# Transposes grouped, two jobs moved to ScalarE, warm matmuls among the first four: a hybrid decoder block in float32

## The chip, the core and the metric

The kernel runs on one core of a Trainium2 chip. The metric is the device time of one execution in microseconds (us). Before the change three runs gave 397.14, 397.4 and 397.8, with a median of 397.4. Below, PE is TensorE, DVE is VectorE, ACT is ScalarE, POOL is GpSimd and SP is SyncE, which issues most transfers.

## What is computed

One decoder layer on 256 tokens of width 1024, in float32. A norm feeds five projections: q, k, v (8 heads of 128), u (512 wide, the input of a state space model) and two gates. Attention is causal within one block of 256. The state space model is a complex diagonal scan with 64 states in each of 32 groups, followed by a gated linear unit (glu). Both branches are gated, summed and projected (wo), and a squared-ReLU MLP (up, down) follows.

```
h = rms_norm(x, norm_mix_g);  q, k, v, u, g = split(h @ w_in)
q, k = rotary(q), rotary(k)
o_a = softmax(mask(q k^T * 128**-0.5)) v
y   = gelu(scan(lambda, B u) C + d_skip * u);  val, gt = split(y @ w_glu);  o_b = val * sigmoid(gt)
x = x + (sigmoid(g_a) * o_a + sigmoid(g_b) * o_b) @ w_out
h = rms_norm(x, norm_mlp_g);  x = x + relu(h @ w_up)**2 @ w_down
return rms_norm(x, norm_final_g)
```

## The kernel before, in words

Every product with a weight is done as three matmuls in the 32-bit replicated format: a weight block `raw` arrives by a transfer on SP's queue, ACT casts it to `hi` (line 83), DVE subtracts to get `lo` (line 84), and PE multiplies hi by the high part of the activations, hi by their low part and lo by their high part (`mm3`, `tok_mm`). There are five raw, four hi and four lo buffers. So each stage is a pipeline SP, ACT, DVE, PE. The stages follow each other: warm matmuls on zeros (`hot`, line 151), the projection u in eight steps k (lines 161 to 183), v, then q, k and the gate for four pairs of heads with attention and the state space model between them (the string `ORDER`), glu, wo, up, down, and the final norm.

Nothing in the source fixes the order of instructions across these parts. A scheduler with a simulated timeline sorts each engine's instructions, with priorities (`tc.high_priority`), and the engines then run their lists strictly in that order. An instruction that waits holds up everything behind it in its engine's list. So an edit in one place can reorder the lists elsewhere.

Names that the later text uses. In the u stage, `xgh` (ACT) and `xgl` (DVE) are the high and low part of the scaled input of a step k, and `hi_u`, `lo_u` the parts of its weights. `par` is a small transfer (128 rows of 60 numbers) with parameters of the state space model; the chain of 128x16 operations that starts on it (`s`, in `prepare`) runs on DVE. `sq` are the squares for the first norm, summed on DVE and then over partitions by the `ms` matmuls; `rs_half` waits for the inverse root that POOL computes. `tables(m)` makes the cosine and sine tables of the scan from a high and a low part of the phase; the low part is added by line 520. `place` (line 455) copies the 16-wide blocks `ab` into the wide matrix `Bs`, whose transposes are `bt`. `s` on PE is the scores' tile (line 307), `pr` the probabilities and `pt` their transposes. `mt` are the transposes of a glu group.

At the end of wo, `x2t` is the residual stream (line 690). For its two column halves c it is transposed (`xt`, line 692, 8 transposes for each half), then ACT writes the scaled high part `x2h` (line 696) and DVE the low part `x2l` (line 697) of each block m, which the matmuls of up read. ACT also sums the squares of x2t (line 700, twice). The two banks of `xt` are used by c=0 and then by c=1, so the second set of transposes waits until x2h and x2l of the first are made.

Of the kernel before, what the change touches and what calls it, by code (L numbers as in the profile page):

```python
# [34 lines left out]

RAW, HI, LO = 5, 4, 4
SPLIT_PRIO = 800
HEAT = 7
RSP = 600
ATT_PRIO = 300  # L40
LAST = 4
# [7 lines left out]
def build(ctx, tc, dr, out):  # L49
# [45 lines left out]
    def behind(ins, others, reason="table set"):  # L95
        for o in others:
            tc.add_manual_dep(ins, o.name, mybir.DependencyInfo(
                mybir.DependencyClass.NoSync, mybir.DependencyReason.DATA), reason=reason)

    def use_set(func):  # L100
# [46 lines left out]
    heat = p1.tile([P, 512], BF16, tag="sw", name="heat")  # L147
    V.memset(heat, 0.0)
    hot = att_bank("hot").rearrange("p a b -> p (a b)")
    for i in range(HEAT):  # L150
# [10 lines left out]
    for c in range(4):  # L161
        wh = keep.tile([P, 1024], F32R, tag="hi", bufs=HI, name=f"hi_u{c}")
        wl = keep.tile([P, 1024], F32R, tag="lo", bufs=LO, name=f"lo_u{c}")
        for k2 in range(2):
            k, cols = 2 * c + k2, slice(k2 * 512, (k2 + 1) * 512)
            xk = xT[:, k, :] if k else x0
            S.activation(xgh[:, k, :], xk, AF.Copy, scale=g_mix[:, k : k + 1])
            V.scalar_tensor_tensor(xgl[:, k, :], xk, g_mix[:, k : k + 1],
                                   xgh[:, k, :].bitcast(F32), op0=ALU.mult, op1=ALU.subtract)
            if k:  # L170
                last = split(wh[:, cols], wl[:, cols], u_raw[c][:, cols])
                if k == 1:
                    second = last
            else:
                for i in range(2):
                    part = slice(i * 256, (i + 1) * 256)
                    split(wh[:, part], wl[:, part], u_raw[c][:, part])
            ws = [slice(k2 * 512 + m * P, k2 * 512 + (m + 1) * P) for m in range(4)]
            for i, (w, x) in enumerate(((wh, xgh), (wh, xgl), (wl, xgh))):
                for m in range(4):  # L180
                    PE.matmul(u_acc[:, m // 2, m % 2, :], w[:, ws[m]], x[:, k, :],
                              start=(k == 0 and i == 0 and m % 2 == 0),
                              stop=(k == KD - 1 and i == 2), skip_group_check=True)
# [19 lines left out]
    ms = att_bank("ms")  # L203
    for h in range(2):
        for i in range(2):
            PE.matmul(ms[:, 0, h : h + 1], sq[:, i, h * P : (h + 1) * P], ones,
                      start=(i == 0), stop=(i == 1))
# [24 lines left out]
    rs_par = rs.rearrange("p (j e) -> p e j", e=2).unsqueeze(1).to_broadcast([P, 2, 2, P])  # L232
    for c in range(2):
        V.tensor_mul(u[:, 2 * c : 2 * c + 2], by_parity(u_acc[:, c]), rs_par)
    V.tensor_mul(rcos, cos_c, rs)
    V.tensor_mul(rsin, sin_c, rs)
    for q in range(4):
        for e in range(2):
            r = 64 * (q % 2) + 32 * e
# [59 lines left out]
        V.tensor_add(o, o, sw)  # L299
        return o  # L300

    scale = P ** -0.5
    mixA = p1.tile([P, KD, T], F32, name="mixA")

    def attn_head(q, k, j):
        s = att_bank("s").rearrange("p a b -> p (a b)")
# [8 lines left out]
        V.tensor_reduce(st[:, 1:2], s[:, 128:384], axis=mybir.AxisListType.X, op=ALU.max)  # L315
        V.tensor_scalar(st[:, 0:2], st[:, 0:2], -scale, None, op0=ALU.mult)
        pr = p1.tile([P, 384], F32, tag="pr", bufs=2, name="pr")
        act(pr[:, 0:128], s[:, 0:128], AF.Exp, bias=st[:, 0:1], scale=scale,
                     accum_out=st[:, 2:3])
        act(pr[:, 128:384], s[:, 128:384], AF.Exp, bias=st[:, 1:2], scale=scale,  # L320
                     accum_out=st[:, 3:4])
        V.reciprocal(st[:, 4:6], st[:, 2:4])
        S.activation(pr[:, 0:128], pr[:, 0:128], AF.Copy, scale=st[:, 4:5])
        S.activation(pr[:, 128:384], pr[:, 128:384], AF.Copy, scale=st[:, 5:6])
        return pr

    def attn_pt(pr):
        pt = att_bank("pt").rearrange("p a b -> p (a b)")
        for i in range(3):
            PE.transpose(pt[:, i * P : (i + 1) * P], pr[:, i * P : (i + 1) * P], ident)  # L330
        pts = p1.tile([P, 384], F32, tag="pts", bufs=2, name="pts")
        S.copy(pts, pt[:, 0:384])
        return pts

    def attn_out(hp, prs, tha):
        pts = [attn_pt(x) for x in prs]
        o = att_bank("o")
        for j in range(2):
            hd = 2 * hp + j
            PE.matmul(o[:, j, :], v[:, 0, hd * P : (hd + 1) * P], pts[j][:, 0:256],  # L340
                      start=True, stop=False, skip_group_check=True)
# [17 lines left out]
    def prepare():  # L359
# [92 lines left out]
        def place(dst, k, src):  # L452
            for g in range(2):
                r = slice(64 * g, 64 * (g + 1))
                G.tensor_scalar(dst[r, :, k + 16 * g : k + 16 * (g + 1)], src[r], 1.0, None,
                                    op0=ALU.mult)
# [54 lines left out]

    def tables(m):
        hi, nlo = ssm[-2:]
        uhi, ang, cs, sn = rot("q", QK), rot("tha", 2), rot("cs", 4), rot("sn", 4)
# [15 lines left out]
    def ssm_quad(m):  # L530
# [29 lines left out]
        V.tensor_sub(sr, sr, w)  # L560
        V.tensor_mul(si, b, sn)
        V.tensor_mul(w, d, cs)
        V.tensor_add(si, si, w)
        Wr, nWi, Dt = ssm[1:4]
        y = bank("y", 1, "y")
        for h in range(2):
            p = 2 * m + h
            PE.matmul(y[:, h, 0:P], Dt[:, p, :], U2[:, p, 1 : P + 1], start=(h == 0), stop=False,
                      skip_group_check=True)
        for i, (w_, s_) in enumerate(((Wr, sr), (nWi, si))):  # L570
            for h in range(2):
                for j in range(2):
                    q = 2 * h + j
                    PE.matmul(y[64 * j : 64 * (j + 1), h, 0:P], w_[:, 4 * m + q, :], s_[:, q, :],
                              start=False, stop=(i == 1), skip_group_check=True)
        if m < 3:
            S.copy(ysb[:, m], y[:, :, 0:P])
        for q in range(4):
# [66 lines left out]
    for q in range(4):  # L645
        acc = wide_banks(f"glu{q}") if q % 2 else [flat(mm_bank(f"glu{q}{h}")) for h in range(2)]
        for kk_ in range(2):
            wh, wl = w_unit(dr["w_glu"][2 * q + kk_], f"glu{q}{kk_}")
            for k2 in range(2):
                k, w = 2 * kk_ + k2, slice(k2 * 512, (k2 + 1) * 512)  # L650
                for hf in range(2):
                    tok_mm(acc[hf], wh[:, w], wl[:, w], yhl[0][:, 0:4], yhl[0][:, 4:8], k, hf,
                           k == 0, k == 3)
        tp = att_bank(f"mt{q}")
        for hf in range(2):
# [4 lines left out]
            V.scalar_tensor_tensor(tb, tb, 1.0, sg, op0=ALU.add, op1=ALU.mult)  # L660
            for i in range(2):
                PE.transpose(tp[:, i, hf * P : (hf + 1) * P], tb[:, i * P : (i + 1) * P], ident)
# [221 lines left out]
```

## Time and profile before

| | |
|---|---|
| median of three runs | 397.4 us |
| the profiled execution | 396.13 us, of which 394.3 are the span |
| PE busy | 384.7 us (98%) |
| DVE busy | 293.0 us (74%) |
| ACT busy | 225.9 us (57%) |
| POOL busy | 30.9 us (8%) |

The profile's stretches show DVE busy for 21.8 of 23 us from 18 to 41, and for 112.6 of 119 us from 41 to 160, and PE for 117.1 of those 119. From 160 to 388.2 PE has no idle time in the view of stretches; the 6.1 us from 388.2 to the end are the final norm and the transfer of the output. A row of the timeline gives the start, the time to the end of the last of a merged group, the engine, the line, the operation, the tiles it writes and reads, the shape and the count, and in brackets the idle time before it with what ended it. Successive instructions on one engine overlap a little, so a group's cost to its engine is the distance between two starts.

### The profile page before, as it was taken

The numbers are of one execution on the slowest core, as the hardware profiler recorded it, in microseconds if no ns is written. First come the engines' busy times: TensorE is split into PE (matmuls) and PEld (weight loads), VectorE is DVE, ScalarE is ACT, GpSimd is POOL, SyncE is SP. The second block draws the span as 40 slices with busy tenths as digits, with TensorE's granted clock in tenths as the row PEclk, the third lists the DMA queues.
The fourth block names the chain that finished last, engine by engine and source line by source line (L and its number), as shares of the span: only waits on it lengthen the run. The fifth ranks groups of instructions, "written<-read, shape, count | busy, mean of one in ns | idle before, by whom it ended". The sixth has DMA issues, their size and how long they took to land.

```text
span 394.3 us, 6719 instructions
## 1 busy us (share of the span) xinstructions
PE 384.7 (98%) x2563; PEld 344.5 (87%) x2563; DVE 293.0 (74%) x521; ACT 225.9 (57%) x360; POOL 30.9 (8%) x39
## 2 busy tenths in 40 slices
PE   8999999999999999999999999999999999999993
PEld 5988898999899787888889999999999888888883
DVE  5989999999999996659748677666676444563434
ACT  6857976664366665945636755655655434344313
POOL 4261491000000000000000000000000000000000
PEclk9999999999999999999999999999999999999998
DMA  8994743354625255347396386656556555565202
GB/s 275 374 342 147 248 161 107 108 173 160 215 72 183 91 166 161 118 152 236 140 324 214 106 267 208 193 185 211 187 190 211 173 204 192 184 211 177 89 2 106
DMA packets 23199, 71.57 MB, mean 181 GB/s; under 512 B 2944, under 2 KB 5248, under 8 KB 23168
## 3 DMA queue, kind: packets, MB, share of 16 engines
q1 hardware_dynamic: 20144, 68.92, 52.5%
q10 hardware_dynamic: 3024, 2.23, 2.0%
q8 instruction: 20, 0.33, 0.3%
q14 instruction: 11, 0.09, 0.1%
HBM read 69.18 MB, written 1.05 MB: 178 GB/s over the span
## 4 chain that ended last, share of the span: by engine, by line
PE 79%; DVE 10%; DMA 3%; issue 3%; ACT 2%; POOL 1%; ACTq 1%; SPq 0%
PE up L90 7%; PE up L89 7%; PE up L88 7%; PE dn L734 6%; PE dn L735 6%; PE dn L736 6%; PE gb L269 2%; PE gb L267 2%; PE gb L268 2%; PE glu L269 2%; PE glu L267 2%; PE wo L268 2%; PE glu L268 2%; PE wo L267 2%; PE wo L269 2%
## 5 line engine op out<-in xcount | busy, mean ns | idle before, releaser
L89 PE MATMUL up<-x2l,hi_up 128*128 128x256 f32 x256 | 70.7, 277 | 0.0
L90 PE MATMUL up<-x2h,lo_up 128*128 128x256 f32 x256 | 70.6, 277 | 0.0
L88 PE MATMUL up<-x2h,hi_up 128*128 128x256 f32 x256 | 70.1, 277 | 0.0
L84 DVE TENSOR_TENSOR lo_dn<-raw_dn,hi_dn 128x1024 fp32r<-128x1024 f32 x32 | 39.2, 1225 | 40.4 <-ACT hi_dn L83 40.4
L83 ACT CAST hi_dn<-raw_dn 128x1024 fp32r<-128x1024 f32 x32 | 33.6, 1049 | 49.1 <-PE dn L736 24.6
L84 DVE TENSOR_TENSOR lo_up<-raw_up,hi_up 128x1024 fp32r<-128x1024 f32 x32 | 38.9, 1225 | 23.7 <-ACT hi_up L83 23.7
L83 ACT CAST hi_up<-raw_up 128x1024 fp32r<-128x1024 f32 x32 | 33.3, 1050 | 35.0 <-PE up L89 16.3
L89 PEld LDWEIGHTS up<-x2l,hi_up 128*128 128x128 f32 x256 | 48.1, 188 | 0.0
L90 PEld LDWEIGHTS up<-x2h,lo_up 128*128 128x128 f32 x256 | 48.1, 188 | 0.0
L88 PEld LDWEIGHTS up<-x2h,hi_up 128*128 128x128 f32 x256 | 47.9, 188 | 0.1
L735 PE MATMUL dn<-lo_dn,hh 128*128 128x512 f32 x96 | 37.4, 390 | 0.0
L736 PE MATMUL dn<-hi_dn,hl 128*128 128x512 f32 x96 | 37.4, 390 | 0.0
L734 PE MATMUL dn<-hi_dn,hh 128*128 128x512 f32 x96 | 37.4, 389 | 0.0
L734 PEld LDWEIGHTS dn<-hi_dn,hh 128*128 128x128 f32 x96 | 18.0, 188 | 3.7
L736 PEld LDWEIGHTS dn<-hi_dn,hl 128*128 128x128 f32 x96 | 18.0, 188 | 3.7
L735 PEld LDWEIGHTS dn<-lo_dn,hh 128*128 128x128 f32 x96 | 18.0, 188 | 3.6
L89 PE MATMUL g<-xgl,hi_g 128*128 128x256 f32 x64 | 18.5, 290 | 0.0
L90 PE MATMUL q<-xgh,lo_q 128*128 128x256 f32 x64 | 18.1, 283 | 0.0
L88 PE MATMUL k<-xgh,hi_k 128*128 128x256 f32 x64 | 18.1, 283 | 0.0
L90 PE MATMUL g<-xgh,lo_g 128*128 128x256 f32 x64 | 18.1, 282 | 0.0
L89 PE MATMUL q<-xgl,hi_q 128*128 128x256 f32 x64 | 18.0, 282 | 0.0
L88 PE MATMUL g<-xgh,hi_g 128*128 128x256 f32 x64 | 18.0, 282 | 0.0
(274 smaller groups left out, 1020.4 us busy)
## 6 DMA issues: line engine op xcount, KB each, us to landing
raw_up<-w_up SPq DMA_DIRECT2D x32, 512.0 KB, 3.4
raw_dn<-w_down SPq DMA_DIRECT2D x32, 512.0 KB, 3.3
raw_v<-w_in SPq DMA_DIRECT2D x8, 512.0 KB, 5.9
raw_q<-w_in SPq DMA_DIRECT2D x8, 512.0 KB, 3.3
raw_k<-w_in SPq DMA_DIRECT2D x8, 512.0 KB, 3.5
raw_g<-w_in SPq DMA_DIRECT2D x8, 512.0 KB, 4.0
raw_gb<-w_in SPq DMA_DIRECT2D x8, 512.0 KB, 3.5
raw_glu<-w_glu SPq DMA_DIRECT2D x8, 512.0 KB, 3.3
```

What stands on the lines that cost most here:

```text
L83: ins = S.copy(hi, x).ins
L84: V.tensor_sub(lo, x, hi.bitcast(F32))
L88: PE.matmul(o, wh, xh, start=first, stop=False, **kw)
L89: PE.matmul(o, wh, xl, start=False, stop=False, **kw)
L90: PE.matmul(o, wl, xh, start=False, stop=last, **kw)
L267: PE.matmul(acc, xh[:, k, rows], wh, start=first, stop=False)
L268: PE.matmul(acc, xh[:, k, rows], wl, start=False, stop=False)
L269: PE.matmul(acc, xl[:, k, rows], wh, start=False, stop=last)
L734: PE.matmul(acc, xh, wh[:, w], start=(k == lead), stop=False, skip_group_check=True)
L735: PE.matmul(acc, xh, wl[:, w], start=False, stop=False, skip_group_check=True)
L736: PE.matmul(acc, xl, wh[:, w], start=False, stop=(k == end), skip_group_check=True)
```

## The change

It has seven parts. (1) One more warm matmul of 512 columns ahead of the u stage, and one of 256, 256, 256 and 128 columns behind each of the first four u matmuls. (2) The transfer of `par` is issued behind the second chunk's input and weights, three transfers later on SP's queue. (3) The squares of the first two input blocks stand behind the cast of the second step's weights, and the `ms` matmuls behind the last u matmul. (4) The rotary tables carry the fourth root of 1/128, so the exponential needs no scale, and the negated maximum comes from the reduction itself: eight small DVE operations go. (5) In `tables`, 16 DVE operations of 128x128 become 16 ACT operations of 128x128 and 4 DVE additions of 128x512. (6) The four copies of `ab` into `Bs` move from POOL to ACT, with high priority. (7) The transposes of a glu group wait for both halves. The lists for the attention's transposes, the pairs' outputs and the y matmuls are cut with `[: hp < 0]` and `[: m < 0]`, which are empty for every hp and m, so no wait is added there.

```diff
-HEAT = 7
+HEAT = 8
+FILL = (256, 256, 256, 128)
...
         if c == 0:
+            use_set(AF.Sin)
+        elif c == 1:
             nc.sync.dma_start(par, dr["par"])
-            use_set(AF.Sin)
...
     for i in range(HEAT):
-        PE.matmul(hot, heat[:, 0:P], heat, start=True, stop=True)
+        hottest = warm(512)
...
+                    if k == 0 and i == 0:
+                        behind(mm, [hottest], "warm matmuls keep their place")
+                        hottest = warm(FILL[m])
+                        behind(hottest, [mm], "warm matmuls keep their place")
...
-        S.activation(sq[:, i, :], xk, AF.Square)
+        behind(S.activation(sq[:, i, :], xk, AF.Square).ins, [second], "weights first")
...
-    V.tensor_mul(rcos, cos_c, rs)
-    V.tensor_mul(rsin, sin_c, rs)
+    V.scalar_tensor_tensor(rcos, cos_c, P ** -0.25, rs, op0=ALU.mult, op1=ALU.mult)
+    V.scalar_tensor_tensor(rsin, sin_c, P ** -0.25, rs, op0=ALU.mult, op1=ALU.mult)
...
-        V.tensor_reduce(st[:, 0:1], s[:, 0:128], axis=mybir.AxisListType.X, op=ALU.max)
-        V.tensor_scalar(st[:, 0:2], st[:, 0:2], -scale, None, op0=ALU.mult)
+        V.tensor_reduce(st[:, 0:1], s[:, 0:128], axis=mybir.AxisListType.X, op=ALU.max,
+                        negate=True)
...
-            place(Bs[c], 32, ab[c])
+            place(Bs[c], 32, ab[c], urgent=True)
...
+            S.activation(ulo[:, q, :], tpos, AF.Copy, scale=nlo[:, 4 * m + q : 4 * m + q + 1])
...
-        for q in range(4):
-            V.scalar_tensor_tensor(ang[:, q, :], tpos, nlo[:, 4 * m + q : 4 * m + q + 1],
-                                   ang[:, q, :], op0=ALU.mult, op1=ALU.add)
+        V.tensor_add(ang, ang, ulo)
...
+        pts = [attn_pt(x, [scaled[2 * hp + j]][: hp < 0]) for j, x in enumerate(prs)]
...
+                after(PE.transpose(tp[:, i, hf * P : (hf + 1) * P],
+                                    tbs[hf][:, i * P : (i + 1) * P], ident).ins,
+                       [merged][: 1], "a group's transposes together")
```

The scheduler's lists change from the u stage to the start of up; from there to the end they are the same. Two places matter to what follows.

On DVE, in the u stage, the list of the kernel before stands like this from the low part of the first input block on:

```order
L168 SCALAR_TENSOR_TENSOR xgl<-xg_64,xgh 128x256
L379 TENSOR_SCALAR s_464<-par 128x16
L384 TENSOR_TENSOR s_587<-par 128x16
L384 TENSOR_TENSOR s_589<-par 128x16
L84 TENSOR_TENSOR lo_u_112<-raw_u_67,hi_u_111 128x256
```

Now the same stretch of DVE, further down, from the second step's weights to the third step's (`raw_u_74` holds the weights of the steps k=2 and k=3):

```order
L85 TENSOR_TENSOR lo_u_113<-raw_u_67,hi_u_112 128x512
L400 TENSOR_SCALAR s_469<-par 128x16
L405 TENSOR_TENSOR s_592<-par 128x16
L405 TENSOR_TENSOR s_594<-par 128x16
L179 SCALAR_TENSOR_TENSOR xgl<-xT,xg_64,xgh 128x256
L400 TENSOR_SCALAR s_471<-s_469 128x16
L405 TENSOR_TENSOR s_596<-s_592,s_594 128x16
L179 SCALAR_TENSOR_TENSOR xgl<-xT,xg_64,xgh 128x256
L398 TENSOR_SCALAR s_473<-s_471 128x16
L452 RECIPROCAL s_591<-s_596 128x16
L204 TENSOR_TENSOR sq<-sq 128x512
L410 SCALAR_TENSOR_TENSOR s_475<-s_473,s_469 128x16
```

One more 128x16 operation follows and then the two `lo_u` of k=2 and k=3. The three reads of `par` have moved from ahead of the first step's weights to ahead of the third step's input.

On PE, at the end of wo, the list of before (`hi_wo_2546`, `lo_wo_2547` are the last weight block of wo, xt_2469 and xt_2470 the two banks of transposes):

```order
L267 MATMUL wo_2489<-hi_wo_2546,mxh 128x512
L692 MATMUL xt_2469<-cst,x2t 128x128 x2
L692 MATMUL xt_2470<-cst,x2t 128x128 x2
L692 MATMUL xt_2469<-cst,x2t 128x128 x2
L692 MATMUL xt_2470<-cst,x2t 128x128 x2
L268 MATMUL wo_2489<-lo_wo_2547,mxh 128x512
L269 MATMUL wo_2489<-hi_wo_2546,mxl 128x512
L267 MATMUL wo_2489<-hi_wo_2546,mxh 128x512
L268 MATMUL wo_2489<-lo_wo_2547,mxh 128x512
L269 MATMUL wo_2489<-hi_wo_2546,mxl 128x512
L267 MATMUL wo_2489<-hi_wo_2546,mxh 128x512
L268 MATMUL wo_2489<-lo_wo_2547,mxh 128x512
```

After one more wo matmul, up begins. Now, on PE:

```order
L283 MATMUL wo_2494<-lo_wo_2552,mxh 128x512
L284 MATMUL wo_2494<-hi_wo_2551,mxl 128x512
L723 MATMUL xt_2474<-cst,x2t 128x128 x2
L723 MATMUL xt_2475<-cst,x2t 128x128 x2
L723 MATMUL xt_2474<-cst,x2t 128x128 x2
L723 MATMUL xt_2475<-cst,x2t 128x128 x2
L89 MATMUL up_2593<-x2h,hi_up_2596 128x256
L89 MATMUL up_2659<-x2h,hi_up_2662 128x256
L90 MATMUL up_2593<-x2l,hi_up_2596 128x256
```

The eight transposes of the first half stood ahead of the last eight wo matmuls and stand behind all of them. Seven more matmuls that read block 0 follow, then two that read x2h of block 1, then four transposes of the second half (xt_2567), which need the bank that x2l of block 1 still reads.

On ACT at the same place, before (the cast is that of the fourth block of up):

```order
L696 ACTIVATE x2h<-xt_2469,par 128x256
L696 ACTIVATE x2h<-xt_2470,par 128x256
L696 ACTIVATE x2h<-xt_2469,par 128x256
L696 ACTIVATE x2h<-xt_2470,par 128x256
L83 CAST hi_up_2663<-raw_up_2661 128x1024
L700 ACTIVATE sq_2389,st_2392<-x2t 128x1024 x2
```

and now:

```order
L84 CAST hi_up_2668<-raw_up_2666 128x1024
L727 ACTIVATE x2h<-xt_2474,par 128x256
L731 ACTIVATE sq_2394,st_2397<-x2t 128x1024
L727 ACTIVATE x2h<-xt_2475,par 128x256
L731 ACTIVATE sq_2394,st_2397<-x2t 128x1024
L727 ACTIVATE x2h<-xt_2474,par 128x256
L727 ACTIVATE x2h<-xt_2475,par 128x256
```

The cast, which needs the buffer that the last wo matmul reads, and the two sums of squares have moved ahead of high parts that stood before them. DVE's list moves in the same way: both x2t operations of the second half and lo_up of the same block, which stood behind three and four x2l, now stand ahead of the first.

## Rows read from the trace of the kernel before

**Rows 1.** The page: busy us by engine, share of the span, instructions.

```profile
PE 384.7 (98%) x2563; PEld 344.5 (87%) x2563; DVE 293.0 (74%) x521; ACT 225.9 (57%) x360; POOL 30.9 (8%) x39
```

**Rows 2.** Waits of PE from 10 to 393 us: line, releaser, us in total, times, longest.

```profile
PE s L307 <- DVE k L299: 0.7, 1, 0.7
PE bt L471 <- POOL Bs L455: 0.7, 1, 0.7
PE pt L330 <- ACT pr L323: 0.5, 1, 0.5
```

**Rows 3.** Timeline of PE, 1 to 19: start, us to last end, operation, idle before.

```profile
1.25 3.17 PE L151 MATMUL hot<-heat 128*128 128x512 bf16 x7 [1.25 <-DVE quarter L158]
...
5.58 0.80 PE L181 MATMUL u_acc<-xgh,hi_u 128*128 128x256 f32 x2 [0.21 <-ACT hi_u L83]
...
10.81 0.62 PE L181 MATMUL u_acc<-xgh,lo_u 128*128 128x256 f32 x4
...
18.07 0.95 PE L206 MATMUL ms<-ones,sq 128*128 128x1 f32 x8
```

**Rows 4.** Timeline of DVE, 3.9 to 11 us.

```profile
5.43 0.17 DVE L379 TENSOR_SCALAR s<-par 128x16 f32<-128x16 f32 x1 [0.99 <-DMA par<-par]
...
7.94 0.88 DVE L168 SCALAR_TENSOR_TENSOR xgl<-xT,xg,xgh 128x256 fp32r<-128x256 f32 x2
8.73 0.17 DVE L377 TENSOR_SCALAR s<-s 128x16 f32<-128x16 f32 x1
8.81 0.69 DVE L189 TENSOR_TENSOR sq<-sq 128x512 f32<-128x512 f32 x1
9.41 0.69 DVE L84 TENSOR_TENSOR lo_u<-raw_u,hi_u 128x512 fp32r<-128x512 f32 x1
```

**Rows 5.** Transfer of par: us from issue to landing.

```profile
DMA to landing us min/median/max: 3.3/3.3/3.3
```

**Rows 6.** Last weight transfer of the second chunk: issue on SP, time to landing.

```profile
L133 SPq DMA_DIRECT2D raw_u<-w_u x1: 359/359/359, 3.6 to 3.6; - x1
...
DMA to landing us min/median/max: 4.8/4.8/4.8
```

**Rows 7.** Timeline of PE, end of wo and start of up.

```profile
209.90 1.03 PE L692 MATMUL xt<-cst,x2t 128*128 128x128 f32 x8
...
212.60 0.40 PE L88 MATMUL up<-x2h,hi_up 128*128 128x256 f32 x2
```

**Rows 8.** Timeline of ACT, the same stretch.

```profile
211.92 0.86 ACT L696 ACTIVATE x2h<-xt,par 128x256 fp32r<-128x256 f32 x2 [0.34 <-DVE x2l L697]
212.84 1.05 ACT L83 CAST hi_up<-raw_up 128x1024 fp32r<-128x1024 f32 x1
213.79 1.05 ACT L700 ACTIVATE sq<-x2t 128x1024 f32<-128x1024 f32 x1
...
214.97 1.06 ACT L700 ACTIVATE sq<-x2t 128x1024 f32<-128x1024 f32 x1
```

**Rows 9.** Timeline of DVE, the same stretch.

```profile
211.41 1.50 DVE L697 SCALAR_TENSOR_TENSOR x2l<-xt,par,x2h 128x256 fp32r<-128x256 f32 x3
212.83 1.28 DVE L690 SCALAR_TENSOR_TENSOR x2t<-wo,x2t 128x512 f32<-128x512 f32 x2
...
214.42 1.22 DVE L84 TENSOR_TENSOR lo_up<-raw_up,hi_up 128x1024 fp32r<-128x1024 f32 x1
```

**Rows 10.** Timeline of DVE, ahead of the rotary result k.

```profile
63.22 1.13 DVE L520 SCALAR_TENSOR_TENSOR tha<-cst,s,tha 128x128 f32<-128x128 f32 x4
64.27 0.68 DVE L299 TENSOR_TENSOR k<-k,sw 128x512 f32<-128x512 f32 x1
```

**Rows 11.** Line 455, placing on POOL: count, ns min/median/max, first and last start.

```profile
L455 POOL TENSOR_SCALAR Bs<-ab x4: 918/1096/2266, 44.5 to 49.2; 64x256 f32<-64x256 f32 x4
```

**Rows 12.** Stretches behind the last matmul: busy by engine, PEclk (granted), DMA share, GB/s.

```profile
388.00:388.50 0.50, 0.22 (x2) 0.02 (x1) 0.24 (x1) 0.00 (x0) 0.00 (x0) 1.00 0.78 287
391.00:392.00 1.00, 0.00 (x0) 0.00 (x0) 0.00 (x0) 0.01 (x1) 0.00 (x0) 0.78 0.36 133
```

More of the change, by code (lines that the diff above doesn't have):

```diff
@@ L98, in behind, with after @@
                 mybir.DependencyClass.NoSync, mybir.DependencyReason.DATA), reason=reason)
+    def after(ins, others, reason):
+        for o in others:
+            tc.add_manual_dep(ins, o.name, mybir.DependencyInfo(
+                mybir.DependencyClass.Sync, mybir.DependencyReason.DATA), reason=reason)
     def use_set(func):
@@ L149, in build, with warm @@
     hot = att_bank("hot").rearrange("p a b -> p (a b)")
+    def warm(n):
+        return PE.matmul(hot[:, 0:n], heat[:, 0:P], heat[:, 0:n], start=True, stop=True).ins
     for i in range(HEAT):
-        PE.matmul(hot, heat[:, 0:P], heat, start=True, stop=True)
+        hottest = warm(512)
     xgh = keep.tile([P, KD, T], F32R, tag="xh", name="xgh")
@@ L180, in build @@
                 for m in range(4):
-                    PE.matmul(u_acc[:, m // 2, m % 2, :], w[:, ws[m]], x[:, k, :],
-                              start=(k == 0 and i == 0 and m % 2 == 0),
-                              stop=(k == KD - 1 and i == 2), skip_group_check=True)
+                    mm = PE.matmul(u_acc[:, m // 2, m % 2, :], w[:, ws[m]], x[:, k, :],
+                                   start=(k == 0 and i == 0 and m % 2 == 0),
+                                   stop=(k == KD - 1 and i == 2), skip_group_check=True).ins
+                    if k == 0 and i == 0:
+                        behind(mm, [hottest], "warm matmuls keep their place")
+                        hottest = warm(FILL[m])
+                        behind(hottest, [mm], "warm matmuls keep their place")
     for i, xk in enumerate((x0, xT[:, 1, :])):
-        S.activation(sq[:, i, :], xk, AF.Square)
+        behind(S.activation(sq[:, i, :], xk, AF.Square).ins, [second], "weights first")
     for c in range(1, 4):
@@ L205, in build @@
         for i in range(2):
-            PE.matmul(ms[:, 0, h : h + 1], sq[:, i, h * P : (h + 1) * P], ones,
-                      start=(i == 0), stop=(i == 1))
+            behind(PE.matmul(ms[:, 0, h : h + 1], sq[:, i, h * P : (h + 1) * P], ones,
+                             start=(i == 0), stop=(i == 1)).ins, [mm], "u first")
     rsm = p1.tile([P, 6], F32, name="rsm")
@@ L323, in attn_head, with attn_pt @@
         S.activation(pr[:, 0:128], pr[:, 0:128], AF.Copy, scale=st[:, 4:5])
-        S.activation(pr[:, 128:384], pr[:, 128:384], AF.Copy, scale=st[:, 5:6])
+        scaled.append(S.activation(pr[:, 128:384], pr[:, 128:384], AF.Copy, scale=st[:, 5:6]).ins)
         return pr
-    def attn_pt(pr):
+    def attn_pt(pr, last):
         pt = att_bank("pt").rearrange("p a b -> p (a b)")
         for i in range(3):
-            PE.transpose(pt[:, i * P : (i + 1) * P], pr[:, i * P : (i + 1) * P], ident)
+            after(PE.transpose(pt[:, i * P : (i + 1) * P], pr[:, i * P : (i + 1) * P], ident).ins,
+                   last, "a head's transposes together")
         pts = p1.tile([P, 384], F32, tag="pts", bufs=2, name="pts")
-        S.copy(pts, pt[:, 0:384])
+        copied.append(S.copy(pts, pt[:, 0:384]).ins)
         return pts
+    copied = []
     def attn_out(hp, prs, tha):
-        pts = [attn_pt(x) for x in prs]
+        pts = [attn_pt(x, [scaled[2 * hp + j]][: hp < 0]) for j, x in enumerate(prs)]
         o = att_bank("o")
@@ L339, in attn_out @@
             hd = 2 * hp + j
-            PE.matmul(o[:, j, :], v[:, 0, hd * P : (hd + 1) * P], pts[j][:, 0:256],
-                      start=True, stop=False, skip_group_check=True)
+            after(PE.matmul(o[:, j, :], v[:, 0, hd * P : (hd + 1) * P], pts[j][:, 0:256],
+                             start=True, stop=False, skip_group_check=True).ins,
+                   copied[-1:][: hp < 0], "a pair's outputs together")
             PE.matmul(o[:, j, 128:256], v[:, 1, hd * P : (hd + 1) * P], pts[j][:, 256:384],
@@ L450, in cmul, with place @@
             (V.tensor_sub if neg_i else V.tensor_add)(o_i, o_i, w)
-        def place(dst, k, src):
+        def place(dst, k, src, urgent=False):
             for g in range(2):
                 r = slice(64 * g, 64 * (g + 1))
-                G.tensor_scalar(dst[r, :, k + 16 * g : k + 16 * (g + 1)], src[r], 1.0, None,
-                                    op0=ALU.mult)
+                to = dst[r, :, k + 16 * g : k + 16 * (g + 1)]
+                if urgent:
+                    with tc.high_priority(ATT_PRIO):
+                        S.copy(to, src[r])
+                else:
+                    G.tensor_scalar(to, src[r], 1.0, None, op0=ALU.mult)
         Bs = [p1.tile([P, ST, 64], F32, tag=f"y{c}", name=f"Bs{c}") for c in range(2)]
@@ L567, in ssm_quad @@
             p = 2 * m + h
-            PE.matmul(y[:, h, 0:P], Dt[:, p, :], U2[:, p, 1 : P + 1], start=(h == 0), stop=False,
-                      skip_group_check=True)
+            after(PE.matmul(y[:, h, 0:P], Dt[:, p, :], U2[:, p, 1 : P + 1], start=(h == 0),
+                             stop=False, skip_group_check=True).ins, [done][: m < 0], "y together")
         for i, (w_, s_) in enumerate(((Wr, sr), (nWi, si))):
@@ L573, in ssm_quad @@
                     q = 2 * h + j
-                    PE.matmul(y[64 * j : 64 * (j + 1), h, 0:P], w_[:, 4 * m + q, :], s_[:, q, :],
-                              start=False, stop=(i == 1), skip_group_check=True)
+                    after(PE.matmul(y[64 * j : 64 * (j + 1), h, 0:P], w_[:, 4 * m + q, :],
+                                     s_[:, q, :], start=False, stop=(i == 1),
+                                     skip_group_check=True).ins, [done][: m < 0], "y together")
         if m < 3:
@@ L659, in build @@
             tb = thb[q][:, hf, :]
-            V.scalar_tensor_tensor(tb, tb, 1.0, sg, op0=ALU.add, op1=ALU.mult)
+            merged = V.scalar_tensor_tensor(tb, tb, 1.0, sg, op0=ALU.add, op1=ALU.mult).ins
+            tbs.append(tb)
+        for hf in range(2):
             for i in range(2):
-                PE.transpose(tp[:, i, hf * P : (hf + 1) * P], tb[:, i * P : (i + 1) * P], ident)
+                after(PE.transpose(tp[:, i, hf * P : (hf + 1) * P],
+                                    tbs[hf][:, i * P : (i + 1) * P], ident).ins,
+                       [merged][: 1], "a group's transposes together")
         two = slice(2 * q, 2 * q + 2)
```

13 lines of the change are left out of this document (8 added, 5 removed).

## The prediction

> **What bounds the kernel now.** I read the page's busy shares first: PE is busy for 384.7 of 394.3 us [rows 1], so the end can move only through what PE waits for, through its rate, and through the tail. Then the waits of PE: behind the start there are three, of 0.7, 0.7 and 0.5 us [rows 2]. The scores wait for DVE's rotary result, the transposes `bt` for POOL's copies into Bs, and the transposes `pt` for ACT; 1.9 us in all. The start comes third, in PE's timeline [rows 3]. Seven warm matmuls of 512 columns take 3.17, about 0.43 each with the last one's way to its end taken off, which is 1.2 GHz; 256 columns would take 0.21. Two short gaps follow, the larger of 0.21. [...] Last I read the timelines of PE, ACT and DVE at the end of wo, because the instruction lists change most there [rows 7 to 9].
>
> **The start.** The added warm matmuls are 512 + 896 columns, 1.2 us of PE at 1.2 GHz. They fill the gaps and for the rest push the u matmuls back, unless they bring the clock up sooner. Neither decides, because DVE does: its list has the three reads of par ahead of xgl for k=2, and par is issued behind the second chunk. When does it land? Its new issue is where the last of the three transfers stood, 3.6 us [rows 6]; with its own 3.3 [rows 5] that is 6.9, the lower bound. But that last transfer, now just ahead of it, landed 4.8 behind its issue, at 8.4 [rows 6]. The three go one place forward and par goes behind them, so I take 8.4, and 8.9 as the upper bound (one place of some 0.5 more). DVE idles until then. It waited 0.99 for par before, too [rows 4], but with nothing urgent behind it. Behind par come nine 128x16 operations (0.08 from one start to the next, about 0.8 with the reciprocal), two xgl (8.73 - 7.94 = 0.79), the sum of squares (9.41 - 8.81 = 0.60) and lo_u (0.69) [rows 4]: 8.4 + 0.8 + 0.79 + 0.60 + 0.69 = 11.3. Before, PE started on this lo_u at 10.81 without waiting [rows 3]. PE then runs as before, so the stage ends 0.5 later. With par at 8.9 it is 1.0; with par at 6.9 DVE is no later than before, and PE can gain at most until lo_u's end of before, 9.41 + 0.69 = 10.1: 0.7. **+0.5, from -0.7 to +1.0.** The moved squares lie in ACT's wait for the same chunk, and the `ms` matmuls stood behind u already.
>
> **Tables and placing.** Four operations of line 520 take 64.27 - 63.22 = 1.05 of DVE, right ahead of the rotary result that the scores wait for [rows 10]. For each of four tables one 128x512 addition takes their place, which I price by the sum at 0.60 [rows 4]: DVE gains 4 x (1.05 - 0.60) = 1.8 up to there, and later eight small operations. ACT gets 16 operations of 128x128 more; it is busy for 57% [rows 1]. With 1.8 less ahead of the rotary result I count that wait of 0.7 as gone, and `pt`'s 0.5 as well, since its scores come earlier and ACT's list behind them is as long. Bounds for both together: 0 to -1.2. The copies into Bs took 0.9 to 2.3 on POOL [rows 11]. On ACT no row has one; it lies between nothing and the cast of 128x1024, eight times the elements, 1.05 [rows 8], and nearer the first. So `bt`'s wait of 0.7 goes. What is late next is q's low part, which DVE's list has later than before, behind the `ab` chain: I give 0.5 back. **-0.2, from -0.7 to 0.** The grouping of transposes is real for the glu groups only. PE's eight xt take 1.03 to their end in one run [rows 7], so a break less in such runs is worth some hundredths: **-0.1** for all of them. The first blocks of wo change their order too, and one operation like x2t on DVE (1.28 for two [rows 9]) may come late: **+0.3, from 0 to 0.6**.
>
> **The end of wo** is the largest term. Zero is the moment at which up could be issued behind the last wo matmul, 212.60 before, when nothing kept it waiting [rows 7]. Before, the transposes had gone at 209.90; behind their 0.85 came eight wo matmuls, 1.85 us, in which x2h and x2l were made. Only then came ACT's cast for up (212.84, that is 0.24 [rows 8]), DVE's x2t (212.83) and lo_up [rows 9]. Now the transposes start at zero. The walk, with the durations of these rows:
> - PE has issued the transposes at 0.85. ACT: the cast, which waits for the last wo matmul, 0.24 to 1.3; then x2h of block 0 (0.47) until 1.7. PE stalls 0.85.
> - Two up matmuls (0.113 each [rows 3]), 1.9. DVE: x2t twice, 0.23 to 1.5; lo_up, behind the cast, 1.4 to 2.65; x2l of block 0 (0.5) until 3.1. PE stalls 1.2.
> - Seven up matmuls, 3.9. ACT: the first sum of squares until 2.8 (213.79 to 214.97 is 1.18 with its read [rows 8]), x2h of block 2, the second sum 3.1 to 4.3, x2h of block 1 until 4.8. PE stalls 0.9.
> - Two up matmuls, 5.1; the second transposes need the bank that x2l of block 1 reads until 5.3. PE stalls 0.2.
>
> The work is the same as before; the cover is gone, and other work of ACT and DVE stands ahead. Sum **+3.2, from 2.1** (the first two stalls alone) **to 3.6** (0.1 more for each release).
>
> Do such stalls cost clock as well? PE's last matmul ended within the half us from 388.0, and the granted clock is still full there and 0.78 only over 391 to 392 [rows 12]. So by the rows a stall of 1.2 costs only itself. [...]
>
> **Sum.** +0.5 - 0.7 - 0.5 - 0.2 - 0.1 + 0.3 + 3.2 = +2.5 us. The profiled execution took 396.13, so 398.6. The median of the runs is 1.27 above it; in their terms the forecast is **399.9**, with a range of its own from 398.2 to 401.8.
>
> **The rivals.**
> - *The start pays: faster, 0.10.* The mechanism is the clock in u. Thirty matmuls stand between 5.58 and 10.81 [rows 3]; with the clock up from the warm matmuls on they take 3.4 and not 5.2, a gain of 1.8. For: PE's gaps are filled. Against: DVE. It decides only if par lands near 6.9 and not 8.4, since lo_u for k=2 otherwise caps it. With the three waits gone and wo at its lower bound: 397.4 - 1.8 - 1.9 - 0.1 + 2.1 = 395.7.
> - *Balanced: 0.15.* Par lands early enough to cost nothing, the clock rises as before, all three waits go, wo costs its lower bound: 397.4 - 1.9 - 0.1 + 2.1 = 397.5. For: DVE is relieved where it is full. Against: three waits must go and no new one may come in the reordered lists between.
> - *The clock falls at wo: slower still, 0.12.* Half the rate for as long as in u costs another 1.8: 401.7. Against: rows 12. [...]
> - *The change doesn't do what it says.* True for the attention's, the pairs' and the y lists, which are empty; it is in the sum, and has no chance of its own.
>
> The likeliest case, with its neighbours of one term more or less, has 0.63. Within 0.2% (0.8 us, what this measurement can tell from no change) I put 0.15, faster 0.10, slower 0.75. For eight in ten the range takes in the slower half of the balanced case and the fallen clock: 397.0 to 401.9.
>
> **What would show it.** Right: DVE idle before the reads of par until near 8.4, the u matmuls' end near 18.6, no wait of the scores, and behind wo three waits of PE of about 1 us, on x2h, x2l and x2h, before up runs. Wrong: if up starts within 0.3 us of the transposes' end, or x2l of block 0 is there less than 2 us behind the last wo matmul, the largest term fails; if the u matmuls run 0.113 apart by 6 us and DVE keeps up, the first rival is right.

## The result and the profile after

The changed kernel takes 402.58 us (median of four runs, 401.87 to 404.68) against 397.27 on the same chip: a ratio of 1.0149, interval 1.0125 to 1.0172. It is slower, as forecast, but by 5.3 us and not 2.5, and it lies outside the range. The profiled execution took 402.54 with a span of 400.7, and PE's last matmul starts 6.42 us later than before (394.36 and 387.94). Runs of the experiments come from several chips, on which the kernel before took 395.97 to 396.27, so ratios are compared.

The page's shares answer to [rows 1]: PE's busy time grew by 1.1, the span by 6.4.

```profile
PE 385.8 (96%) x2568; PEld 345.6 (86%) x2568; DVE 289.9 (72%) x501; ACT 232.4 (58%) x380; POOL 29.5 (7%) x35
```

The waits of PE (line, releaser, us in total, times, longest) answer to [rows 2]. None of the three old waits is left. There are eight others (the first warm matmul's 1.2, as before, is left out), and one of 3.3 us behind wo leads.

```profile
PE up L90 <- DVE x2l L728: 3.3, 1, 3.3
...
PE o L360 <- ACT pts L350: 0.9, 1, 0.9
PE u_acc L192 <- ACT hi_u L84: 0.8, 1, 0.8
PE u_acc L192 <- DVE lo_u L85: 0.8, 1, 0.8
PE gb L282 <- DVE q L312: 0.6, 1, 0.6
PE up L89 <- ACT x2h L727: 0.6, 1, 0.6
PE q L91 <- DVE lo_q L85: 0.3, 1, 0.3
PE wo L284 <- DVE mxl L85: 0.3, 1, 0.3
```

**The start.** PE's timeline answers to [rows 3]. From 6.69 to 7.14 four u matmuls stand 0.11 apart; before, thirty of them had taken 0.17 each on average between 5.58 and 10.81, and the 64 behind those, to 18.07, 0.113 each. So the full rate came earlier in this execution. But PE then waits twice, for ACT and for DVE, and `ms` starts 1.29 later. Two v matmuls (0.45) now stand ahead of it, so the loss is 0.84.

```profile
6.69 0.62 PE L192 MATMUL u_acc<-xgh,lo_u 128*128 128x256 f32 x4
7.14 0.62 PE L192 MATMUL u_acc<-xgh,hi_u 128*128 128x256 f32 x4
...
9.47 0.73 PE L192 MATMUL u_acc<-xgh,hi_u 128*128 128x256 f32 x4 [0.81 <-ACT hi_u L84]
...
11.46 0.74 PE L192 MATMUL u_acc<-xgh,lo_u 128*128 128x256 f32 x4 [0.80 <-DVE lo_u L85]
...
19.36 0.95 PE L221 MATMUL ms<-ones,sq 128*128 128x1 f32 x8
```

DVE in the same stretch answers to [rows 4 to 6]. It idles for ACT and then for par until 8.57, and the low part of k=2, the first of the two in the last row, starts at 10.72 and ends near 11.4; the prediction had 8.4 and an end at 11.3. PE goes on with it at 11.46, against 10.81 before.

```profile
7.00 0.69 DVE L85 TENSOR_TENSOR lo_u<-raw_u,hi_u 128x512 fp32r<-128x512 f32 x1 [1.43 <-ACT hi_u L84]
8.57 0.17 DVE L400 TENSOR_SCALAR s<-par 128x16 f32<-128x16 f32 x1 [0.88 <-DMA par<-par]
...
10.72 1.29 DVE L85 TENSOR_TENSOR lo_u<-raw_u,hi_u 128x512 fp32r<-128x512 f32 x2
```

**The end of wo.** PE's timeline answers to [rows 7]. Behind the eight transposes PE could issue up at 213.10 (0.85 behind their start), against 212.60 before, and starts it at 213.92. After two matmuls it stands until 217.70, and the next ones are 0.21 apart, against the 0.11 of the start.

```profile
212.25 1.10 PE L723 MATMUL xt<-cst,x2t 128*128 128x128 f32 x8
213.92 0.50 PE L89 MATMUL up<-x2h,hi_up 128*128 128x256 f32 x2 [0.57 <-ACT x2h L727]
217.70 0.58 PE L90 MATMUL up<-x2l,hi_up 128*128 128x256 f32 x1 [3.27 <-DVE x2l L728]
218.08 0.42 PE L91 MATMUL up<-x2h,lo_up 128*128 128x256 f32 x1
218.29 0.41 PE L89 MATMUL up<-x2h,hi_up 128*128 128x256 f32 x1
```

The stretches show the same by the granted clock (the number behind the five busy times): 0.78 in the us in which the stall ends, then half until 221.

```profile
217.00:218.00 1.00, 0.30 (x1) 0.30 (x2) 1.00 (x3) 1.00 (x3) 0.00 (x0) 0.78 0.73 274
218.00:219.00 1.00, 1.00 (x6) 1.00 (x6) 0.87 (x5) 0.83 (x4) 0.00 (x0) 0.50 0.75 225
...
220.00:221.00 1.00, 1.00 (x6) 1.00 (x6) 0.00 (x0) 0.12 (x1) 0.00 (x0) 0.52 0.52 209
```

DVE answers to [rows 9] and names the origin. It waits 4.76 us for the residual's transfer x2t; only then come the two sums, two low parts, two more sums, one more low part, and x2l last. Before, the first sums had run at 206.52, waiting only for PE.

```profile
211.36 1.29 DVE L721 SCALAR_TENSOR_TENSOR x2t<-wo,x2t 128x512 f32<-128x512 f32 x2 [4.76 <-DMA x2t<-x]
212.56 2.36 DVE L85 TENSOR_TENSOR lo_up<-raw_up,hi_up 128x1024 fp32r<-128x1024 f32 x2
214.83 1.29 DVE L721 SCALAR_TENSOR_TENSOR x2t<-wo,x2t 128x512 f32<-128x512 f32 x2
...
217.16 0.88 DVE L728 SCALAR_TENSOR_TENSOR x2l<-xt,par,x2h 128x256 fp32r<-128x256 f32 x2
```

Why is x2t late? Its buffer is one of the first phase, free once `mixA`'s last parts are read, and those wait for the last glu transposes. The last read, the low part `mxl` on DVE, ends at 202.20 here and at 199.02 before, and SP issues x2t 0.1 us behind it in both. Three rows of after: these transposes on PE, the issue on SP, and the transfer (KB, us to landing).

```profile
199.09 0.60 PE L691 MATMUL mt<-cst,thb 128*128 128x128 f32 x4
```

```profile
202.28 0.39 SPq L703 DMA_DIRECT2D x2t<-x  x1
```

```profile
x2t<-x SPq DMA_DIRECT2D x1, 1024.0 KB, 9.0
```

And the first two of before:

```profile
194.89 0.60 PE L662 MATMUL mt<-cst,thb 128*128 128x128 f32 x4
```

```profile
199.11 0.39 SPq L672 DMA_DIRECT2D x2t<-x  x1
```

The transposes' input is ready at 195.66, but PE now runs them behind 40 matmuls of wo and no longer behind 24, as the two timelines count: 4.2 later. The issue is 3.2 later and the flight 1.7 longer (7.3 before).

The ledger of PE's 6.42: start 0.84; from there to the end of the transposes -0.34 (213.10 - 212.60 is 0.50 in all); first stall 0.82 (213.92 - 213.10); second stall 3.55 (217.70 less 213.92 and two matmuls); the half clock and the rest 1.55. The last three make 5.92 for the end of wo. The profiled execution of before lies 1.1 us below its median and that of after at its own, so the ledger holds 6.4 and the medians 5.3.

### The profile page after: what moved, and what is told of

The parts are those of the page before. It is cut to its first block, busy times and chain, and to the rows that moved or that the text cites. A ratio compares the mean times of both kernels' runs of the same rounds, so it can differ in the third digit from the quotient of the medians.

```text
span 400.7 us, 6723 instructions
## 1 busy us (share of the span) xinstructions
PE 385.8 (96%) x2568; PEld 345.6 (86%) x2568; DVE 289.9 (72%) x501; ACT 232.4 (58%) x380; POOL 29.5 (7%) x35
## 4 chain that ended last, share of the span: by engine, by line
PE 78%; DVE 9%; DMA 4%; ACT 3%; issue 3%; POOL 1%; ACTq 1%; SPq 0%; DVEq 0%
PE up L90 7%; PE up L91 7%; PE up L89 7%; PE dn L767 5%; PE dn L765 5%; PE dn L766 5%; DMA x2t<-x 2%; PE q L91 2%; PE gb L282 2%; PE q L89 2%; PE q L90 2%; PE gb L284 2%; PE gb L283 2%; PE glu L282 2%; PE glu L284 2%
## 5 line engine op out<-in xcount | busy, mean ns | idle before, releaser
L90 PE MATMUL up<-x2l,hi_up 128*128 128x256 f32 x256 | 71.7, 280 | 3.3 <-DVE x2l L728 3.3
L89 PE MATMUL q<-xgh,hi_q 128*128 128x256 f32 x64 | 18.3, 286 | 0.0
L91 PE MATMUL k<-xgh,lo_k 128*128 128x256 f32 x64 | 18.2, 284 | 0.0
```

The lines of the kernel that those rows point to most:

```text
L89: PE.matmul(o, wh, xh, start=first, stop=False, **kw)
L90: PE.matmul(o, wh, xl, start=False, stop=False, **kw)
L91: PE.matmul(o, wl, xh, start=False, stop=last, **kw)
```

## The experiments

Theory: the last glu transposes stand late in PE's list; x2t lands late, PE stalls, and its clock falls. Rivals: the late par and the warm matmuls at the start; the transposes of x2t behind wo, which by themselves leave up uncovered; merging itself.

**e1: the last transposes early.** In the changed kernel, one matmul of wo is put behind the last glu transposes:

```diff
+                    if c == 1 and k == 0 and hf == 1:
+                        behind(lead[-1], mts[-4:], "last glu transposes first")
```

> The changed kernel, with one added order: in wo's second column half the second matmul of the first weight block stands behind the last glu group's transposes. The lists up to there are those of the changed kernel. Theory A (the residual's transfer is late because the last glu transposes stand some 15 matmuls late in PE's list, so that the memory it needs is released late, and DVE's list waits for it): those transposes go from 199.1 to about 196, the transfer is issued near 199 instead of 202.3, up starts without the 3.3 us wait and at the full clock, and the time falls by 5.5 to 6.3 us to 396.3 to 397.1. Rival B (the loss lies in the u stage and in ACT's added work): it falls by less than 1.5 us, to 401 or more.

Measured 397.83 (seven runs, 396.6 to 401.43), ratio 1.0057 (1.0024 to 1.0091). The last transposes start near 196.3, x2t is issued at 199.25 and flies 7.0, and the wait for x2l before up is gone; the longest wait left there is this one.

```profile
PE xt L727 <- DVE x2l L732: 0.6, 1, 0.6
```

By the ratios about 3.7 us come back, for the theory and against the rivals at the start, which are unchanged here. The median stays above the expected range; the profiled execution was the fastest of the seven, and what the slower ones wait for isn't seen. The edit also brings eight transposes of x2t ahead of the last wo matmuls again, so it doesn't part a late x2t from a missing cover; for that see e5.

**e2: SP's order alone.** The residual goes ahead of the weights `up11`:

```diff
+        if name == "up11":
+            behind(got, [xload], "residual first")
```

> The changed kernel with two transfers exchanged on SP's queue, and nothing else in any list: the residual stands ahead of the fourth weight block of up, as in the kernel before. Theory A: its issue stays at 202.3, since it waits there for memory, but its flight of 9.0 us shortens by what the 512 KB ahead of it took, some 1.2 us; the wait of up's third matmul (3.3) shortens by as much, and the time falls by 0.8 to 1.5 us to 401.1 to 401.8. If the exchange of the two transfers were the cause, the flight would go back to 7.3 and the time would fall by 3 us or more. If the landing did not matter (the order of ACT's and DVE's lists behind the transposes alone, as in the prediction), the time stays at 402.6.

Measured 401.85, ratio 1.0129 (1.0093 to 1.0165). The flight is 8.0, up waits 2.4 and not 3.3. By the ratios that is 0.8 us less, the lower edge of the theory's range, and the intervals overlap: a small part at most.

**e3: the clock alone.** 28 matmuls of 256 columns into a spare bank fill the second stall; they add work and leave none out.

```diff
+                for _ in range(28):
+                    fill = PE.matmul(spare[:, 0, :], w[0], xh, start=True, stop=True).ins
```

> The changed kernel with 28 matmuls of 256 columns into a spare bank between the first two matmuls of up, where PE idles for 3.3 us; the lists of the other engines are the same. They are work that is not needed. Theory A with the clock: the granted clock stays at its upper level, the matmuls from 217.7 to 221 go at 0.113 and not at 0.21, and the time falls by 1.2 to 1.8 us to 400.8 to 401.4. If the fallen clock costs nothing (the work behind it waits for other things anyway), the time stays at 402.6 or rises by up to 0.3.

Measured 401.19, ratio 1.012 (1.010 to 1.0141): some 1.1 us less than the change, just short of the 1.2 expected, and the intervals overlap. The granted clock stays full where it had been half; PE's end is 5.41 behind before and not 6.42. Counted from the start of the eight transposes (212.79 here), PE's last matmul comes 1.55 earlier than in the changed kernel, all that the ledger had for the half clock and the rest.

```profile
218.00:219.00 1.00, 1.00 (x11) 1.00 (x9) 0.86 (x4) 1.00 (x4) 0.00 (x0) 1.00 1.06 352
```

**e4: par early, all else as changed.**

```diff
         if c == 0:
+            nc.sync.dma_start(par, dr["par"])
             use_set(AF.Sin)
-        elif c == 1:
-            nc.sync.dma_start(par, dr["par"])
```

> The changed kernel with the transfer of par issued where it was before, behind the first chunk. The scheduler then writes the end of wo as in the kernel before. Theory A: the wait of DVE for par (0.88) goes, the low part of k=2 is ready near 10.2, the u stage ends near 17.6 instead of 19.3, and with the end of wo restored the time is 394.5 to 396.3. Rival C (warm matmuls among the first four cost as much as they bring): the u stage ends no earlier than before, 18.1, and the time is 396.5 to 397.3.

Measured 395.15, ratio 0.9977 (0.9965 to 0.999): this version beats the kernel before by a little. On the scale of the result's 397.27 that is 396.4, between the two forecasts; u ends 0.2 earlier than before and not 0.5. The scheduler also writes the end of wo as before, so two causes go at once.

```profile
PE v L282 <- DVE lo_v L85: 0.8, 1, 0.8
PE up L90 <- DVE x2l L727: 0.7, 1, 0.7
```

**e5 and e6: the gain of the last norm later.** Its 512 KB are issued at the same moment as x2t. In e5 (the changed kernel) and e6 (e4's version) they go behind the fifth pair of up:

```diff
-    nc.scalar.dma_start(gfin, dr["gfin"].partition_broadcast(P))
...
+        if i == 4:
+            behind(nc.scalar.dma_start(gfin, dr["gfin"].partition_broadcast(P)).ins, [made],
```

> The changed kernel with one transfer moved: the 512 KB gain of the last norm is issued on ACT's queue behind the fifth up pair and no longer at the end of wo, where its issue fell at the same moment as that of x2t; all other lists are as in the changed kernel. Theory: x2t is late by 3.2 because of its issue and by 1.7 because the two transfers share the DMA engines, so its flight falls from 9.0 to about 7.0 us, x2l of block 0 comes 2 us earlier, PE's stall of 3.3 falls to 1.3, and the clock does not fall: 2.0 + 0.8 to 1.6 less, a ratio of 1.004 to 1.009 to the kernel before. Rival: the flight is set by SP's queue and the weights on it; it stays near 9 us and the ratio between 1.012 and 1.017.

Measured 400.74, ratio 1.0121 (1.0074 to 1.0167). The flight fell to 6.9, as the theory has it, x2t landed at 208.4, and the second stall shrank:

```profile
211.46 1.03 PE L723 MATMUL xt<-cst,x2t 128*128 128x128 f32 x8
213.13 0.50 PE L89 MATMUL up<-x2h,hi_up 128*128 128x256 f32 x2 [0.64 <-ACT x2h L727]
214.82 0.39 PE L90 MATMUL up<-x2l,hi_up 128*128 128x256 f32 x1 [1.19 <-DVE x2l L728]
```

But the clock fell all the same, after three stretches with PE half busy or less, and the ratio misses the expected range:

```profile
212.00:213.00 1.00, 0.50 (x5) 0.26 (x3) 1.00 (x3) 1.00 (x3) 0.00 (x0) 1.00 0.64 246
213.00:214.00 1.00, 0.50 (x2) 0.30 (x2) 1.00 (x2) 1.00 (x3) 0.00 (x0) 1.00 0.98 324
214.00:215.00 1.00, 0.18 (x1) 0.18 (x2) 1.00 (x3) 1.00 (x4) 0.00 (x0) 1.00 0.85 250
...
217.00:218.00 1.00, 1.00 (x7) 1.00 (x6) 0.13 (x1) 0.47 (x1) 0.00 (x0) 0.50 0.59 238
```

This is the prediction's own walk with x2t in time: stalls of 0.82 (213.13 less 211.46 and 0.85) and 1.46 (214.82 less 213.13 and two matmuls), against 0.85 and 1.2. Counted from the end of the transposes (212.31), PE's last matmul, at 392.17, comes 4.52 later than before and not 5.92, so some 1.4 us go with the late landing. Of the 4.52, some 1.3 are the clock: the thirteen matmuls from 217.34 to 220.12 took 2.78, and at 0.113 each they would have taken 1.5. The other 3.2 us are the uncovered transposes, as the prediction walked them. So the rival that these transposes leave up uncovered holds for about half of the loss at the end of wo. The split is read from two executions; the medians can't show it.

> The same move of the gain in the version with par issued early, which is 0.9977 of the kernel before. There x2t flew 9.5 us and up waited 0.7 for x2l. Theory: the flight falls by about 2, that wait goes, and nothing else does: 0.6 to 1.0 less, a ratio of 0.995 to 0.9965. Rival (another of DVE's operations is next in line, or the flight does not depend on the gain): 0.997 to 0.999.

Measured 395.41, ratio 0.9982 (0.9959 to 1.0005). The flight fell from 9.5 to 8.0 and the wait for x2l is gone, but v waits 1.2 and not 0.8, u 0.8 and not 0.2. The ratio lies where the rival had it, and in time e6 can't be told from e4.

**e7: not merged.** Each half's glu transposes wait for their own half:

```diff
-        for hf in range(2):
             for i in range(2):
-                after(PE.transpose(tp[:, i, hf * P : (hf + 1) * P],
-                                    tbs[hf][:, i * P : (i + 1) * P], ident).ins,
-                       [merged][: 1], "a group's transposes together")
+                PE.transpose(tp[:, i, hf * P : (hf + 1) * P], tb[:, i * P : (i + 1) * P], ident)
```

> The changed kernel with the glu groups' transposes not merged: those of the first half wait only for the first half, as before. The list of PE keeps the late place of the last group, behind 43 rows and not 28, and so its late x2t. Theory: the place in PE's list makes the loss and not the merging, so the last group still ends near 199, x2t lands near 211, up waits more than 2 us for x2l, and the ratio stays between 1.011 and 1.018. Rival (the wait for the second half, which merging adds, makes the loss): the group ends near 196, and the ratio is 1.002 to 1.007.

Measured 405.81, ratio 1.0234 (1.0183 to 1.0286), slower still, and above both ranges. The last transposes start near 201, x2t lands at 213.21, and PE waits for it twice. So the late place is there without the merging, too, and with it the loss.

```profile
PE up L90 <- DVE x2l L723: 2.4, 1, 2.4
PE xt L718 <- DVE x2t L716: 1.4, 1, 1.4
```

**e8: par late, alone.** The kernel before with only that edit:

```diff
         if c == 0:
-            nc.sync.dma_start(par, dr["par"])
             use_set(AF.Sin)
+        elif c == 1:
+            nc.sync.dma_start(par, dr["par"])
```

> The kernel before with par alone issued late, behind the second chunk of the input weights, as in the change; no more warm matmuls. Theory: par lands near 8.5, DVE idles for it until then, low parts of k=2 and k=3 come late, and the u matmuls end 0.6 to 1.3 later than the 18.07 of before; with the end of wo in the order of before the ratio is 1.001 to 1.005. Rival (the start's loss comes from the warm matmuls and the moved weights, not from par): the u matmuls end within 0.3 of before, and the ratio is 0.998 to 1.001.

Measured 406.86, ratio 1.0267 (1.0224 to 1.0311): far beyond both. DVE reads par from 8.05 on, and u ended 0.65 later, as the theory said; v starts only 0.20 later. The loss stands at 164 to 173, where the transposes of the last probabilities wait for ACT. Its list puts a table load, yT and thb between the last head's exponentials and its scaling:

```profile
PE pt L331 <- ACT pr L324: 7.6, 2, 4.8
```

```profile
168.02 1.28 ACT L101 ACT_TABLE_LOAD   x1
169.31 1.33 ACT L107 ACTIVATE yT<-yT 128x256 f32<-128x256 f32 x4
170.55 1.54 ACT L107 ACTIVATE thb<-gb,rs_half 128x256 f32<-128x256 f32 x4
```

**e9 to e11: e4's version less one part.** e9 without the added warm matmuls, e10 with the copies into Bs on POOL, e11 with the tables' low part on DVE:

```diff
-HEAT = 8
+HEAT = 7
```

> The version with par issued early (0.9977 of the kernel before), with only the seven warm matmuls of before: the eighth and the four among the first u matmuls are gone. Theory: with par out of the way the warm matmuls are what pays in it, since the clock then rises near 5.6 us and later, as before, and not near 4.9; the u matmuls end 0.2 to 0.8 later than in that version (18.3 to 19.0), and the ratio is 0.999 to 1.002. Rival (DVE's low parts set u's pace with or without a full clock): u ends within 0.2 of it, and the ratio stays at 0.996 to 0.9985.

Measured 398.59, ratio 1.0054 (1.0028 to 1.008). The u matmuls end 1.4 later than in e4, in an execution that was the slowest of twelve; both are more than expected. The moments that the expectation gave for the clock were off: by their distances the u matmuls reach full rate near 5.2 here without the added warm matmuls, near 7.0 in e4, and near 6.4 in the changed kernel. But then PE waits 1.1 and 0.4 for lo_u, and the clock falls once more and stays down until 11; in e4 it does not:

```profile
8.00:9.00 1.00, 1.00 (x5) 1.00 (x6) 1.00 (x6) 1.00 (x3) 0.00 (x0) 0.50 1.03 397
```

That could speak for the warm matmuls, if not by the way expected. But DVE also read par later here than in e4, at 6.4 and not at 5.7, ahead of those low parts, so it isn't shown; the lists behind differ too, with waits of 1.7 (y) and 1.4 (pt).

```diff
-            place(Bs[c], 32, ab[c], urgent=True)
+            place(Bs[c], 32, ab[c])
```

> The version with par issued early, with the copies into Bs back on POOL. Theory (the prediction's term for them): the wait of the transposes bt for POOL comes back with 0.4 to 0.7, the ratio is 0.9985 to 1.0005. Rival (the wait is covered or turns into one for another engine): 0.996 to 0.9985, and no wait of bt for POOL.

Measured 403.0, ratio 1.0154 (1.0115 to 1.0193). The wait for POOL came back with 0.4, near the prediction's term for it. The ratio is far above both ranges, since the time went elsewhere: as in e8, ACT's list puts yT and thb ahead of the last head's scaling.

```profile
PE pt L346 <- ACT pr L339: 6.1, 1, 6.1
...
PE bt L495 <- POOL Bs L480: 0.4, 1, 0.4
```

```diff
-        V.tensor_add(ang, ang, ulo)
+        for q in range(4):
+            V.scalar_tensor_tensor(ang[:, q, :], tpos, nlo[:, 4 * m + q : 4 * m + q + 1],
+                                   ang[:, q, :], op0=ALU.mult, op1=ALU.add)
```

> The version with par issued early, with the phases' low part back on DVE as four operations of 128x128 and no sum. Theory (the prediction's term for the tables): DVE is later by 0.45 per table ahead of the rotary result, and the scores' wait for it comes back with 0.3 to 1.0; the ratio is 0.999 to 1.001. Rival (the scores had other work of PE ahead of them): no wait of s, ratio 0.996 to 0.9985.

Measured 392.77, ratio 0.9898 (0.9867 to 0.9929), the fastest of all, below both ranges. No wait of the scores came back, as the rival had it, and behind the start PE hardly waits at all:

```profile
PE u_acc L191 <- DVE lo_u L85: 0.6, 2, 0.4
PE up L90 <- DVE x2l L727: 0.3, 1, 0.3
```

**e12: tables on DVE, par late.** e11's edit on the changed kernel, so that e11 and e12 differ only in par's issue.

> The changed kernel with the tables' low part back on DVE alone (four operations of 128x128 for the sum); par stays late. With the same edit and par early the time was 0.9898 of the kernel before. In the list of PE the last glu group stands behind 28 rows again, as before, so x2t is early. Theory: the end of wo costs no stall above 1 us; par late costs 0.6 to 1.3 at u, as in the other runs with par late; the ratio is 0.992 to 0.997. Rival (the late par shifts the lists in the middle, as it did alone): another wait of 1 to 8 us stands in the attention, the u matmuls are no later than in the changed kernel, and the ratio is 1.002 to 1.02.

Measured 398.54, ratio 1.0064 (1.0041 to 1.0087): the rival's size. Without v's two matmuls, u's last matmul starts at 18.53 here and at 18.50 in e11. So between these two executions par's late issue costs nothing at u; it costs through the lists behind, here a wait of pt (and, at the start, a wait for hi_u that e11 lacks). Over all executions with the added warm matmuls, u ends 0.7 later than before on average with par late (seven, from 0.1 to 1.1) and 0.1 later with par early (four, from -0.2 to 0.5).

```profile
PE pt L347 <- ACT pr L340: 1.1, 1, 1.1
PE u_acc L192 <- ACT hi_u L84: 1.0, 2, 0.8
```

## Why the prediction was wrong

- **The start** (+0.5, bounds -0.7 to +1.0): measured 0.84. The mechanism held: DVE capped u. Its low part of k=2 ended at 11.4 for the 11.3 summed, PE went on 0.65 later than before, and the run behind that took 0.19 more. PE's wait of 0.81 for the cast lies ahead of this one and is not in the loss. That the added warm matmuls brought the clock up earlier isn't shown: e8 and e9 have only the seven of before, and e8 has 32 matmuls in 4.28 us of busy PE from 5 to 10, where the kernel before has 25 in 4.79; by their distances the u matmuls reach full rate near 5.2 in e9 and near 7.0 in e4, which has them all. The prediction's 1.2 GHz is 512 columns in 0.43 us [rows 3], an estimate; the runs show distances and granted shares, no frequency.
- **The three waits** (-0.7, -0.5, -0.2): all gone, as forecast. But waits for pts, q, lo_q and mxl came, 2.1 in all, for which the sum had only a part (0.5 ahead of q and 0.3 at wo). From the start to the end of the transposes the gain was 0.34 and not 1.2. The waits by themselves make a loss of 0.2 (2.1 less 1.9); the half us that PE gained besides lies in no listed wait. It may be the shorter runs of grouped transposes, for which the sum had 0.1; no run shows it.
- **The end of wo** (+3.2) is the step that failed; it measured 5.92. Its first stall was right, 0.82 for 0.85. For the second, the walk begins with "x2t twice, 0.23 to 1.5", bound only to ACT and PE. I had taken the residual's transfer as landed, as before, and had not followed PE's list back to the last glu transposes nor SP's to x2t. Instead of 1.2 the stall took 3.55; the later stalls of 0.9 and 0.2 did not come. Of the 2.7 us beyond the forecast some 1.4 go with that late landing (5.92 less e5's 4.52) and the rest with the clock, which the sum had at nothing. e1 moves the place in PE's list and takes back 3.7 us, with the cover of the transposes in it; e7 shows that merging as such isn't needed for the late place; and in e5, with x2t in time, the walk's stalls are 0.82 and 1.46.
- **The clock.** I held the fall at wo to be a rival of 0.12, because [rows 12] show a full clock behind the last matmul and 0.78 only some 3 us later. Those rows have one idle stretch; wo has several with a few matmuls between. No row of before shows that several such stalls cost clock. The clock fell in the changed kernel, with 0.50 granted over 218 to 220, behind the stall, while PE was fully busy again, and 1.00 from 221 on; and it fell, after stalls hardly longer than forecast, in e5, with 0.50 over 217 to 220. It cost 1.55 by e3 and some 1.3 in e5, for the rival's 1.8. So the rival belonged into the main case: e5's ratio on 397.4 is 402.2, near the rival's 401.7.
- **What stays open:** why the scheduler puts the last glu transposes 16 matmuls later wasn't tried in isolation. Undoing par's move (e4) or the tables (e12) brings the old place back, while undoing the merging (e7) doesn't; so it seems to hang on timings far ahead, and no single part is shown to be its cause. For the same reason the single edits' own prices can't be read from e8 to e12.

## What to carry to other kernels

Where a scheduler writes the lists, an edit's own price (here 0.2 to 1 us) is the smaller part; look in each engine's new list for the last producer ahead of every stage's start, and follow it back through the transfers, with the moment at which their buffers come free, before the stage's work is walked. Price short stalls that follow each other with the clock as well (here 1.55 us by e3 and some 1.3 in e5). And try parts of a bundle: par early and the tables on DVE, with the other parts kept, was 1% faster than before, the whole 1.5% slower.

## What the hardware showed that was not expected

- The granted clock fell to half where PE's longest wait was 2.4 (e2) to 6.1 us (e10), but also at the end of wo in e5, where none was above 1.2; in e4, where PE was 0.69 and 0.64 busy in two stretches of one us, it stayed full.
- A 1 MB transfer took 6.9 to 9.5 us to land; moving a 512 KB one that was issued together with it shortened it from 9.0 to 6.9 and from 9.5 to 8.0.
- At the start the granted clock can't be read from the view of stretches: in the kernel before it is 1.00 from the first us on, as in the row below, while the u matmuls there stand 0.21 apart up to 9.2 and 0.11 only from then on. Go by the distances there.

```profile
7.00:8.00 1.00, 1.00 (x7) 1.00 (x6) 1.00 (x6) 0.96 (x3) 0.00 (x0) 1.00 1.01 338
```
